# A two-layer stream encoder on one core: the end of the last token tile, with x loaded earlier on another queue, the sample's tokens on four quadrants, and the last stores on other queues

## The chip, the cores and the metric

The kernel runs on one core of a Trainium2 chip. The metric is the device time of one execution in microseconds. The core's engines appear in the profile as PE (TensorE, with PEld for its weight loads), DVE (VectorE), ACT (ScalarE), POOL (GpSimd) and SP (SyncE, which here only issues transfers). All arithmetic is in float32; a matrix product is made of three products of split halves.

## The reference, cut to what matters

Two layers (a gated chunk mixer, then a pooling mixer), each followed by a squared-ReLU channel MLP. The same weights serve 1024 prompt tokens and 32 sample tokens of width 1024; the MLP is 4096 wide. The end of the second layer is what the change touches.

```
h = rmsnorm(x, g_norm[i, 2]) * (1 + sc2) + sh2
f = square(relu(h @ ffn_w_up[i])) @ ffn_w_down[i]
x = x + gt2 * rmsnorm(f, g_norm[i, 3])          # the output, after the last layer
```

## The kernel before, in words

The tokens lie in three tiles: 0 and 1 have 384 prompt tokens each, tile 2 has 256 prompt tokens and the 32 of the sample, 288 columns. Activations are channel-major: `acc[t]` is 128 partitions x 8 channel blocks x the tile's tokens, and `A(t, d)` is one block of it.

The MLP's 4096 hidden channels go in eight chunks of 512. `ffn_item(p, t, after)` is one chunk for one tile. It has four `up(j)`, each a PSUM tile `pf` of 24 products, ReLU and square on ACT, and a split into `fh` (ACT) and `fl` (DVE); and a `down()` with eight groups `pg`, d = 0 to 7, of 12 products each. `accumulate(t, d, ...)` adds each group to `acc` on DVE. `pf` has two PSUM banks (`ps_up`), `pg` three (`ps_dn`), the small sums have `ps_ms`. A `down()` is held back (`pending`) until the next item's first `up` is out. In the last layer the chunks 4 and 5 run over all tiles, then 6 and 7 over tiles 0 and 1, then 6 and 7 over tile 2 alone, so the kernel ends with chunk 7 of tile 2. Weights are loaded on SP's queue into three `raw` buffers, copied by ACT to the high part (`wh`, L422) and subtracted by DVE to the low part (`wl`, L79, the line of the helper behind every DVE add, subtract and multiply-add).

In chunk 7 each accumulated block is squared (`Stat.square`, L750) for the norm. Tiles 0 and 1 are then finished by fillers, generators that a planner (`weave`) advances between groups while its sum of DVE times is behind its sum of PE times: `residual` scales and adds x (`xo_r`), then eight DVE transposes of 32x32 blocks go to `turned` (L1617), each followed by four stores of 48 KB (L1619). Of these q = 3 is on POOL's queue, the others are on SP's.

Tile 2 has an end of its own. `scale_last(d)` multiplies block d by the gate's coefficient on ACT (L1360); at d = 0 it issues nine loads of the tile's x on SP's queue (L1349), from `xsd`, a copy in DRAM, into the room `l0`; and at d = 3, 4, 5 it turns x on DVE (L1355) into the room `h0`, which `turned0` had before. `turn_last(d)` transposes block d on PE (L1368) into `yT`: the two prompt blocks of 128 tokens, and a third that ends with the sample's 32. Behind the last group `last()` makes the norm's sums in `pn_last` with the squares as weights (L1574), then 1/sqrt with one Newton step in three small DVE operations, and six multiply-adds out = yT * r + x, four of 128x512 and two of 32x512. After each comes its store on SP's queue (L1602).

A scheduler puts the instructions of each engine into one fixed list when the program is built; on the chip each engine runs its list in order. Transfers issued by SP and ACT share eight completion semaphores, handed round in the order of the list, and a transfer waits until the one that had its semaphore before it has landed.

Of the kernel before, what the change touches and what calls it, by code (L numbers as in the profile page):

```python
# [15 lines left out]
P = 128  # L16
# [18 lines left out]
def tile_stream_encoder_step(  # L35
# [1088 lines left out]
    def accumulate(t, d, ps, first):  # L1124
        n = ncol[t]
        if first:
            act(out=A(t, d), in_=ps[:, :n], func=AF.Copy)
        else:
            tt(out=A(t, d), in0=A(t, d), in1=ps[:, :n], op=ALU.add)

    def up_terms(wkey, t):
        wh, wl = need_w(wkey)
# [150 lines left out]
    def ffn_item(p, t, after):  # L1283
        l, c, tiles = passes[p]
        last = t == tiles[-1]
        n = ncol[t]
        hid = []

        def up(j):
            ps = ps_up(f"pf{l}_{c}_{t}_{j}")  # L1290
            products(ps, n, up_terms(("up", p, j), t))
            if last:
                w_finish(("up", p, j))
            r = t_m(f"r{l}_{c}_{t}_{j}")
            act(out=r[:, :n], in_=ps[:, :n], func=AF.Relu)  # L1295
            a, b = t_hid("h", f"fh{l}_{c}_{t}_{j}"), t_hid("l", f"fl{l}_{c}_{t}_{j}")
            act(out=r[:, :n], in_=r[:, :n], func=AF.Square)
            split(a, b, r, n)
            hid.append((a, b))

        def down():
            for d in range(KB):
                ps = ps_dn(f"pg{l}_{c}_{t}_{d}")
                wh, wl = need_w(("dn", p, d // 2))
                terms = []
                for j in range(4):
                    o = j * 256 + (d % 2) * P
                    a, b = hid[j]
                    terms.append((wh[:, o : o + P], wl[:, o : o + P], a[:, :n], b[:, :n]))
                products(ps, n, terms)  # L1310
                accumulate(t, d, ps, c == 0)
                if d == 0 and after is not None:
                    st = Stat(t, f"rf{l}_{t}", l == 0 or t < NT - 1)
                if after is not None:
                    st.square(d)
                    if l == 1 and t == NT - 1:
                        scale_last(d)
                        if d in (2, 4, 6):
                            turn_last(d - 2)
                            turn_last(d - 1)  # L1320
                if last and d % 2 == 1:
                    w_finish(("dn", p, d // 2))
                weave(d % 2)
            if after is not None:
                after(st)

        for j in range(4):
            up(j)
            weave()
            if j == 0:  # L1330
                flush()
        pending.append(down)
# [1 line left out]

    last_ps = {}

    def scale_last(d):
        t = NT - 1
        if d == 0:
            last_ps["x"], last_ps["raw"] = (  # L1340
                room(part, 0, f"xlast_{part}").rearrange("p k n -> p (k n)").rearrange(
                    "p (b d) -> p b d", d=D
                )
                for part in "hl"
            )
            src = xsd.rearrange("c k q n -> c (k q) n")
            for i, (c0, r0, nr) in enumerate(LAST):
                for r1 in range(r0, r0 + nr, DEC):
                    nc.sync.dma_start(  # L1349
                        last_ps["raw"][r1 : r1 + DEC, i, :].rearrange("p (m n) -> p m n", n=DEC),  # L1350
                        src[:, :, c0 + r1 : c0 + r1 + DEC],
                    )
        if d in (3, 4, 5):
            i, r0, nr = d - 3, LAST[d - 3][1], LAST[d - 3][2]
            nc.vector.transpose(  # L1355
                out=last_ps["x"][r0 : r0 + nr, i, :], in_=last_ps["raw"][r0 : r0 + nr, i, :]
            )
        for c0, w, v in segs[t]:
            a = A(t, d, c0, w)
            act(out=a, in_=a, func=AF.Copy, scale=coef[:, 1, 3, v, d : d + 1])  # L1360

    def turn_last(d):
        half = d // 4
        for i, (c0, _, _) in enumerate(LAST):
            if d % 4 == 0:
                take = ps_up if half == 0 and i < 2 else (ps_ms if half == 0 or i < 2 else ps_dn)
                last_ps[(i, half)] = take(f"yT{i}_{half}")
            nc.tensor.transpose(  # L1368
                last_ps[(i, half)][:, (d % 4) * P : (d % 4 + 1) * P], A(NT - 1, d, c0, P), ident
            )  # L1370

    def mix_to_ffn(st, l):
        t = st.t
# [182 lines left out]
    def to_out(st):  # L1556
        t = st.t
        col0, npr, nsm = TILES[t]
        blocks = [
            (c * P, P, y_prompt[0, col0 + c * P : col0 + (c + 1) * P, :]) for c in range(npr // P)  # L1560
        ]
        if nsm:
            blocks.append((npr, nsm, y_sample[0]))

        def last():

            turn_last(KB - 2)
            pn = ps_dn("pn_last")
            nb = len(LAST)
            for k in (0, KB - 1):  # L1570
                if k > 0:
                    turn_last(KB - 1)
                for i, (c0, _, _) in enumerate(LAST):
                    mm(  # L1574
                        pn[:, 2 * i : 2 * i + 2],
                        st.sq[:, k, c0 : c0 + P],
                        ones[:, 0:2],
                        start=k == 0 and i == 0,
                        stop=k > 0 and i == nb - 1,
                        skip_group_check=True,  # L1580
                    )
            sums = pn[:, : 2 * nb].rearrange("p (b c) -> p b c", c=2)[:, :, 0]
            r, q = (t_st(f"{x}_last")[:, :nb] for x in ("r", "q"))
            act(out=r, in_=sums, func=AF.Abs_reciprocal_sqrt, scale=1.0 / D)
# [4 lines left out]
            dsts = [dst for _, _, dst in blocks]  # L1589
            for i, (_, r0, nr) in enumerate(LAST):  # L1590
                rows = slice(r0, r0 + nr)
                for half in range(2):
                    d = slice(half * 512, half * 512 + 512)
                    stt(
                        out=xt[rows, i, d],
                        in0=last_ps[(i, half)][rows, :],
                        scalar=r[rows, i : i + 1],
                        in1=xt[rows, i, d],
                        op0=ALU.mult,
                        op1=ALU.add,  # L1600
                    )
                    nc.sync.dma_start(dsts[i][:, d], xt[rows, i, d])  # L1602
            yield False

        def run():
            need_ada(1, 5)
            if t == NT - 1:
                yield from last()
                return
            yield from residual(st, 1, 3, f"r2_1_{t}", [], store=False, stat=False)  # L1610
            turned = room("h", t, f"turned{t}")
            dst = y_prompt[0, col0 : col0 + npr, :].rearrange(
                "(b i) (k q c) -> q k i b c", i=DEC, q=P // DEC, c=DEC
            )
            for k in range(KB):
                time["dve"] += 0.1 + npr / 930.0
                nc.vector.transpose(out=turned[:, k, :], in_=A(t, k))  # L1617
                for q in range(P // DEC):
                    (nc.gpsimd if q == 3 else nc.sync).dma_start(  # L1619
                        dst[q, k],  # L1620
                        turned[DEC * q : DEC * (q + 1), k, :].rearrange("p (b c) -> p b c", c=DEC),
                    )
                yield False

        fillers.append((f"out_{t}", run()))
# [48 lines left out]
```

## Time and profile before

| | us |
|---|---|
| median of three runs | 2172.68 (2172.60, 2172.68, 2174.59) |
| profiled execution | 2173.74 |
| its span | 2171.7 |
| mean granted clock of TensorE | 0.996 |
| busy: PE, DVE, ACT, POOL | 2145.5, 1431.8, 971.3, 13.3 |
| last product of the MLP starts | 2158.75 |
| last multiply-adds start | 2167.11 |

The profiled execution's own time has 2.04 us outside the span, and lies 1.06 above the median. All positions are microseconds from the span's start, in that one execution. In a timeline row the columns are start, duration, engine, line, operation, out<-in with shapes, and the count of instructions that the row joins; a bracket gives the idle time before it and what ended it.

### The profile page before, as it was taken

How to read it: one execution, taken by the hardware profiler on the slowest of the kernel's cores; microseconds unless marked ns; L12 is line 12 of the kernel's file. 1: busy time of each engine (PE TensorE's matmuls, PEld its weight loads, DVE VectorE, ACT ScalarE, POOL GpSimd, SP SyncE). 2: the span in 40 equal slices, each digit the busy share in tenths (PEclk: the TensorE clock that was granted, in tenths of full speed). 3: DMA queues.
4: the chain of work that ended last, by engine and by line, in shares of the span. 5: the costliest groups of instructions: out<-in, count | busy, mean ns of one | idle time of the engine just before them, and what ended most of it. 6: DMA issues, size and time to landing. Idle time of an engine off the chain costs nothing.

```text
span 2171.7 us, 33210 instructions
## 1 busy us (share of the span) xinstructions
PE 2145.5 (99%) x13214; PEld 2078.1 (96%) x13214; DVE 1431.8 (66%) x2499; ACT 971.3 (45%) x1643; POOL 13.3 (1%) x30
## 2 busy tenths in 40 slices
PE   7999999999999999999999999999999999999998
PEld 5778899999999999999999999999999999999997
DVE  5688647566879548496747879869675554523377
ACT  4633422234447552323445566666555542313354
POOL 0000000000000000000000000000000000000001
PEclk9999999999999999999999999999999999999999
DMA  8386534343437454243645466565455552302255
GB/s 300 119 269 193 173 93 139 90 148 109 147 96 233 132 155 143 87 140 110 196 129 161 141 189 182 171 191 158 141 161 158 157 155 68 98 20 78 69 139 125
DMA packets 383262, 312.95 MB, mean 144 GB/s; under 512 B 39458, under 2 KB 346346, under 8 KB 383108
## 3 DMA queue, kind: packets, MB, share of 16 engines
q1 hardware_dynamic: 380452, 308.64, 46.8%
q8 instruction: 103, 1.69, 0.3%
q10 hardware_dynamic: 2144, 1.41, 0.2%
q0 software_dynamic: 512, 0.79, 0.1%
q14 instruction: 51, 0.42, 0.1%
HBM read 278.95 MB, written 31.84 MB: 143 GB/s over the span
## 4 chain that ended last, share of the span: by engine, by line
PE 93%; DVE 3%; DMA 2%; ACT 1%; issue 1%; ACTq 0%; DVEq 0%; SPq 0%
PE pg L902 11%; PE pg L903 11%; PE pg L904 11%; PE pf L902 11%; PE pf L904 11%; PE pf L903 11%; PE po L902 3%; PE po L903 3%; PE po L904 3%; PE pu L902 3%; PE pu L904 3%; PE pu L903 3%; PE pv L929 2%; PE pv L930 2%; PE pv L931 2%; PE pp L1532 1%
## 5 line engine op out<-in xcount | busy, mean ns | idle before, releaser
L902 PE MATMUL pg<-fh,wh_dn 128*128 128x384 f32 (+1 forms) x1536 | 495.8, 323 | 0.0
L902 PE MATMUL pf<-hh,wh_up 128*128 128x384 f32 (+1 forms) x1536 | 494.4, 322 | 0.0
L903 PE MATMUL pf<-hl,wh_up 128*128 128x384 f32 (+1 forms) x1536 | 493.1, 321 | 0.0
L904 PE MATMUL pf<-hh,wl_up 128*128 128x384 f32 (+1 forms) x1536 | 492.9, 321 | 0.2 <-DVE wl_up L79 0.2
L903 PE MATMUL pg<-fl,wh_dn 128*128 128x384 f32 (+1 forms) x1536 | 492.6, 321 | 0.4 <-DVE fl L79 0.4
L904 PE MATMUL pg<-fh,wl_dn 128*128 128x384 f32 (+1 forms) x1536 | 492.5, 321 | 0.0
L79 DVE TENSOR_TENSOR wl_up<-raw,wh_up 128x1024 fp32r<-128x1024 f32 x152 | 185.9, 1224 | 165.4 <-ACT wh_up L422 165.4
L902 PEld LDWEIGHTS pg<-fh,wh_dn 128*128 128x128 f32 x1536 | 288.3, 188 | 1.5 <-ACT fh L1121 0.6
L903 PEld LDWEIGHTS pg<-fl,wh_dn 128*128 128x128 f32 x1536 | 288.3, 188 | 1.5 <-DVE fl L79 0.7
L904 PEld LDWEIGHTS pf<-hh,wl_up 128*128 128x128 f32 x1536 | 288.6, 188 | 0.5 <-DVE wl_up L79 0.5
L903 PEld LDWEIGHTS pf<-hl,wh_up 128*128 128x128 f32 x1536 | 288.3, 188 | 0.4
L902 PEld LDWEIGHTS pf<-hh,wh_up 128*128 128x128 f32 x1536 | 288.2, 188 | 0.4
L904 PEld LDWEIGHTS pg<-fh,wl_dn 128*128 128x128 f32 x1536 | 288.3, 188 | 0.0
L422 ACT ACTIVATE wh_up<-raw 128x1024 fp32r<-128x1024 f32 x152 | 161.2, 1060 | 279.9 <-PE pf L903 213.6
L79 DVE TENSOR_TENSOR acc<-acc,pg 128x384 f32<-128x384 f32 (+1 forms) x336 | 174.2, 519 | 146.3 <-PE pg L904 145.7
L422 ACT ACTIVATE wh_dn<-raw 128x1024 fp32r<-128x1024 f32 x152 | 160.8, 1059 | 202.9 <-PE pg L903 170.6
L79 DVE TENSOR_TENSOR wl_dn<-raw,wh_dn 128x1024 fp32r<-128x1024 f32 x152 | 186.0, 1224 | 82.4 <-ACT wh_dn L422 82.2
L79 DVE SCALAR_TENSOR_TENSOR aa<-raw,csil,aa 128x512 f32<-128x512 f32 (+1 forms) x364 | 203.5, 623 | 8.0 <-DMA raw<-in_w_ada_dram 7.9
L1295 ACT ACTIVATE r<-pf 128x384 f32<-128x384 f32 (+1 forms) x192 | 86.6, 451 | 201.9 <-PE pf L904 199.2
L79 DVE TENSOR_TENSOR fl<-r,fh 128x384 fp32r<-128x384 f32 (+1 forms) x192 | 100.3, 523 | 85.4 <-ACT fh L1121 84.3
L902 PE MATMUL pu<-hh,wh_u 128*128 128x384 f32 (+1 forms) x384 | 125.8, 328 | 0.0
L902 PE MATMUL po<-ush,wh_o 128*128 128x384 f32 (+1 forms) x384 | 123.5, 322 | 0.0
(263 smaller groups left out, 2927.2 us busy)
## 6 DMA issues: line engine op xcount, KB each, us to landing
raw<-in_ffn_w_up_dram SPq DMA_DIRECT2D x152, 512.0 KB, 3.9
raw<-in_ffn_w_down_dram SPq DMA_DIRECT2D x152, 512.0 KB, 3.5
raw<-in_w_ada_dram SPq DMA_DIRECT2D x96, 512.0 KB, 4.3
raw<-in_sgu_w_in_dram SPq DMA_DIRECT2D x40, 512.0 KB, 4.4
xd<-acc SPq DMA_DIRECT2D x8, 1536.0 KB, 7.8
raw<-in_sgu_w_out_dram SPq DMA_DIRECT2D x24, 512.0 KB, 4.0
xo_r<-xd SPq DMA_DIRECT2D x32, 384.0 KB, 3.4
vd<-vt SPq DMA_DIRECT2D x32, 256.0 KB, 4.5
```

The lines of the kernel that those rows point to most:

```text
L79: return op(out, *args, **kw)
L422: act(out=wh, in_=r, func=AF.Copy)
L902: mm(ps[:, :n], wh, rh, start=i == 0, stop=False)
L903: mm(ps[:, :n], wh, rl, start=False, stop=False)
L904: mm(ps[:, :n], wl, rh, start=False, stop=i == last)
L929: mm(ps[:m, :], a_h, wh[:, o : o + 512], start=k == 0, stop=False)
L930: mm(ps[:m, :], a_h, wl[:, o : o + 512], start=False, stop=False)
L931: mm(ps[:m, :], a_l, wh[:, o : o + 512], start=False, stop=k == KB - 1)
L1295: act(out=r[:, :n], in_=ps[:, :n], func=AF.Relu)
L1532: mm(ps[:, :n], wg[:, k, e * P : (e + 1) * P], A(t, 2 * g + k), start=k == 0, stop=k == 1)
```

## The change

- `load_last(j)` is new: in chunk 6 of tile 2, after each `up(j)`, ACT's queue issues three of twelve loads of x (eight of 32 blocks, four of 8 blocks for the sample) into the room `l0`. The sample's 32 tokens are laid out on four quadrants of 32 partitions, 256 channels each.
- x is turned into the room `l1` instead of `h0`, by three DVE transposes (128x1024 twice, 128x256) that are set behind the accumulations d = 1, 2, 3.
- `turn_last` transposes two blocks of 128 tokens instead of three; the sample's 32 columns become weights of a matmul with the identity, which lands on quadrant d // 2 of one PSUM tile `yTs`.
- The norm's sums for the sample are made on each of the four quadrants, and its two multiply-adds of 32x512 become one of 128x256. The last block is turned behind the sums of both squares (k = 0 and 7) instead of between them.
- The scaling of the block d = 7 is on DVE instead of ACT.
- The four large last stores are on ACT's queue; the sample's are four of 32x256, alternately on SP's and ACT's.
- Tile 0's stores of q = 2 move from SP's queue to POOL's.

The core of the diff:

```diff
-    LAST = [(0, 0, P), (P, 0, P), (ncol[-1] - P, P - DEC, DEC)]
+    LAST = (0, P)
...
     def accumulate(t, d, ps, first):
...
+        return tt(out=A(t, d), in0=A(t, d), in1=ps[:, :n], op=ALU.add)
...
-                accumulate(t, d, ps, c == 0)
+                done = accumulate(t, d, ps, c == 0)
...
-                        scale_last(d)
+                        scale_last(d, done.ins)
...
         for j in range(4):
             up(j)
+            if l == 1 and c == 6 and t == NT - 1:
+                load_last(j)
             weave()
...
+    def load_last(j):
+        if j == 0:
+            last_ps["raw"] = room("l", 0, "xlast_l").rearrange("p k n -> p (k n)")
+        raw = last_ps["raw"]
+        src = xsd.rearrange("c k q n -> c (k q) n")
+        parts = [
+            (i * D, DEC, r1, slice(0, DEC), c0 + r1)
+            for i, c0 in enumerate(LAST)
+            for r1 in range(0, P, DEC)
+        ]
+        parts += [
+            (2 * D, 8, DEC * g, slice(8 * g, 8 * g + 8), TILES[-1][1]) for g in range(P // DEC)
+        ]
+        for at, m, r1, ms, n0 in parts[3 * j : 3 * j + 3]:
+            nc.scalar.dma_start(
+                raw[r1 : r1 + DEC, at : at + m * DEC].rearrange("p (m n) -> p m n", n=DEC),
+                src[:, ms, n0 : n0 + DEC],
+            )
...
+    def scale_last(d, done):
         t = NT - 1
         if d == 0:
...
-                    nc.sync.dma_start(
-                        last_ps["raw"][r1 : r1 + DEC, i, :].rearrange("p (m n) -> p m n", n=DEC),
-                        src[:, :, c0 + r1 : c0 + r1 + DEC],
-                    )
-        if d in (3, 4, 5):
...
+            last_ps["x"] = room("l", 1, "xlast_h").rearrange("p k n -> p (k n)")
+        if d in (1, 2, 3):
+            c = slice((d - 1) * D, min(d * D, 2 * D + 256))
+            with tc.issue_after(done):
+                nc.vector.transpose(out=last_ps["x"][:, c], in_=last_ps["raw"][:, c])
+        if d == KB - 1:
+            for c0, w, v in segs[t]:
+                a = A(t, d, c0, w)
+                ts(a, a, coef[:, 1, 3, v, d : d + 1], None, op0=ALU.mult)
+            return
...
     def turn_last(d):
...
+        if d == 0:
+            last_ps["s"] = ps_ms("yTs")
+        q = d // 2 * DEC
+        mm(
+            last_ps["s"][q : q + DEC, d % 2 * P : d % 2 * P + P],
+            A(NT - 1, d, TILES[-1][1], DEC),
+            ident,
+            start=True,
+            stop=True,
+            tile_position=(0, q),
+            skip_group_check=True,
+        )
...
             for k in (0, KB - 1):
-                if k > 0:
-                    turn_last(KB - 1)
-                for i, (c0, _, _) in enumerate(LAST):
+                for i in range(2):
                     mm(
                         pn[:, 2 * i : 2 * i + 2],
...
+                for q in range(0, P, DEC):
+                    mm(
+                        pn[q : q + DEC, 4:6],
+                        st.sq[:, k, npr:],
+                        ones[:, 0:2],
+                        start=False,
+                        stop=k > 0,
+                        tile_position=(0, q),
+                        skip_group_check=True,
+                    )
+            turn_last(KB - 1)
...
+            for i in range(2):
                 for half in range(2):
...
-                    nc.sync.dma_start(dsts[i][:, d], xt[rows, i, d])
+                    nc.scalar.dma_start(blocks[i][2][:, d], x)
+            x = xt[:, 2 * D : 2 * D + 256]
+            stt(
+                out=x,
+                in0=last_ps["s"][:, :256],
+                scalar=r[:, 2:3],
+                in1=x,
+                op0=ALU.mult,
+                op1=ALU.add,
+            )
+            for g in range(P // DEC):
+                (nc.scalar if g % 2 else nc.sync).dma_start(
+                    blocks[2][2][:, g * 256 : (g + 1) * 256], x[DEC * g : DEC * (g + 1), :]
+                )
...
-                    (nc.gpsimd if q == 3 else nc.sync).dma_start(
+                    (nc.gpsimd if q > 1 + t else nc.sync).dma_start(
```

More of the change, by code (lines that the diff above doesn't have):

```diff
@@ L1126, in accumulate @@
         if first:
-            act(out=A(t, d), in_=ps[:, :n], func=AF.Copy)
-        else:
-            tt(out=A(t, d), in0=A(t, d), in1=ps[:, :n], op=ALU.add)
+            return act(out=A(t, d), in_=ps[:, :n], func=AF.Copy)
+        return tt(out=A(t, d), in0=A(t, d), in1=ps[:, :n], op=ALU.add)
     def up_terms(wkey, t):
@@ L1363, in turn_last @@
         half = d // 4
-        for i, (c0, _, _) in enumerate(LAST):
+        for i, c0 in enumerate(LAST):
             if d % 4 == 0:
-                take = ps_up if half == 0 and i < 2 else (ps_ms if half == 0 or i < 2 else ps_dn)
-                last_ps[(i, half)] = take(f"yT{i}_{half}")
+                last_ps[(i, half)] = (ps_up if half == 0 else ps_ms)(f"yT{i}_{half}")
             nc.tensor.transpose(
```

37 lines of the change are left out of this document (10 added, 27 removed).

## The prediction

> **What bounds the kernel now.** I read the page first: its busy times, then the chain that ended last.
>
> ```profile
> span 2171.7 us, 33210 instructions
> PE 2145.5 (99%) x13214; PEld 2078.1 (96%) x13214; DVE 1431.8 (66%) x2499; ACT 971.3 (45%) x1643; POOL 13.3 (1%) x30
> PE 93%; DVE 3%; DMA 2%; ACT 1%; issue 1%; ACTq 0%; DVEq 0%; SPq 0%
> ```
>
> TensorE (PE) is busy for 99% of the span and carries 93% of the chain. So an edit counts only where it makes PE wait, or behind PE's last product. The change touches the last 90 us, so next come windows of that stretch. The columns are the length, then the busy time and count of PE, PEld, DVE, ACT and POOL, then clock, DMA share and GB/s.
>
> ```profile
> 2085.00:2108.40 23.40, 23.40 (x142) 23.40 (x141) 22.80 (x36) 13.42 (x24) 0.00 (x0) 1.00 0.68 191
> 2108.40:2127.50 19.10, 19.10 (x145) 19.10 (x145) 15.48 (x26) 12.04 (x20) 5.07 (x8) 1.00 0.90 216
> 2127.50:2143.70 16.20, 16.20 (x124) 16.20 (x123) 14.56 (x27) 4.57 (x9) 1.50 (x3) 1.00 0.43 95
> 2143.70:2159.00 15.30, 15.30 (x118) 14.87 (x118) 10.04 (x19) 10.31 (x25) 3.45 (x6) 1.00 0.69 119
> 2159.00:2171.70 12.70, 2.15 (x19) 1.82 (x17) 7.58 (x12) 1.34 (x4) 0.00 (x0) 0.65 0.25 93
> ```
>
> PE is full to 2159.0 at 0.13 us a product (19.10 / 145, 288 columns each). DVE is nearly full to 2143.7 and looser after. The last 12.7 us are a tail in which PE does little. The timeline of that tail:
>
> ```profile
> 2158.75 0.29 PE L904 MATMUL pg<-fh,wl_dn 128*128 128x288 f32 x1
> 2159.08 0.45 DVE L79 TENSOR_TENSOR acc<-acc,pg 128x288 f32<-128x288 f32 x1 [0.81 <-PE pg L904]
> 2159.21 1.69 PE L1574 MATMUL pn_last<-ones,sq_rf 128*128 128x2 f32 x12
> 2160.93 0.17 ACT L1584 ACTIVATE r_last<-pn_last 128x3 f32<-128x3 f32 x1 [0.17 <-PE pn_last L1574]
> 2161.80 1.41 DVE L79 SCALAR_TENSOR_TENSOR xlast_h<-yT,r_last,xlast_h 128x512 f32<-128x512 f32 x2
> 2163.13 1.23 DVE L1355 STREAM_TRANSPOSE xlast_h<-xlast_l 128x1024 f32<-128x1024 f32 x1
> 2164.40 1.41 DVE L79 SCALAR_TENSOR_TENSOR xlast_h<-yT,r_last,xlast_h 128x512 f32<-128x512 f32 x2
> 2165.84 1.24 DVE L1355 STREAM_TRANSPOSE xlast_h<-xlast_l 32x1024 f32<-32x1024 f32 x1
> 2167.11 1.44 DVE L79 SCALAR_TENSOR_TENSOR xlast_h<-yT,r_last,xlast_h 32x512 f32<-32x512 f32 x2
> ```
>
> After PE's last product come one accumulation, the norm, and then six final multiply-adds with two transposes of x between them, all on DVE: 2161.80 to 2168.55, that is 6.75 us. The last store and the close take the remaining 3.15 us.
>
> **The tail on DVE: -3.7 us.** The two transposes (1.27 us each by starts) move ahead of the last product, and the sample's two multiply-adds on 32 partitions become one on 128x256. The four big ones keep 0.665 us each ((2163.13 - 2161.80) / 2). The 128x256 one is estimated at 0.42, below the 0.53 that 384 columns take in the next fence. Sum 4 x 0.665 + 0.42 = 3.08 instead of 6.75. Bounds -3.5 and -3.8, by that one estimate.
>
> **DVE before the last product: +2.0 us.** The transposes are not free where they go. Worse, the order of PE's products changes. In the list of the changed kernel, the chunk 6 down groups of the last tile are interleaved with chunk 7's up groups, and the first of the eight groups becomes complete only 141 products after 2108.41, at about 2127.5 (141 x 0.132 plus pauses). DVE's next instruction is that group's accumulation, so DVE stands idle from about 2122.1, with the weights' low parts (wl_up, wl_dn) and tile 1's residual queued behind it. What it then does, by start-to-start times:
>
> ```profile
> 2129.65 0.45 DVE L79 TENSOR_TENSOR acc<-acc,pg 128x288 f32<-128x288 f32 x1
> 2130.02 0.55 DVE L79 SCALAR_TENSOR_TENSOR r_rf<-q_rf,r_rf 128x384 f32<-128x384 f32 x1
> 2130.49 1.22 DVE L79 TENSOR_TENSOR wl_dn<-raw,wh_dn 128x1024 fp32r<-128x1024 f32 x1
> 2131.62 0.45 DVE L79 TENSOR_TENSOR acc<-acc,pg 128x288 f32<-128x288 f32 x1
> 2131.99 1.15 DVE L79 SCALAR_TENSOR_TENSOR acc<-acc,coef,r_rf 128x384 f32<-128x384 f32 x2
> 2133.05 0.45 DVE L79 TENSOR_TENSOR acc<-acc,pg 128x288 f32<-128x288 f32 x1
> 2136.35 0.95 DVE L79 TENSOR_TENSOR acc<-acc,xo_r 128x768 f32<-128x768 f32 x1
> 2137.22 1.14 DVE L79 SCALAR_TENSOR_TENSOR acc<-acc,coef,r_rf 128x384 f32<-128x384 f32 x2
> 2140.05 2.41 DVE L1617 STREAM_TRANSPOSE turned<-acc 128x384 f32<-128x384 f32 x5
> 2146.46 0.46 DVE L79 TENSOR_TENSOR acc<-acc,pg 128x288 f32<-128x288 f32 x1 [0.62 <-PE pg L904]
> ```
>
> Each 288-column add takes 0.37, a 1024-column subtract 1.13, a 384-column multiply-add 0.53, a 768-column add 0.87 and a turned transpose 0.48. The changed list has, from 2127.5 to chunk 7's first accumulation, 12, 6, 10, 4 and 2 of these: 4.4 + 6.8 + 5.3 + 3.5 + 1.0 = 21.0 us. With 0.8 for waits the first accumulation ends at 2149.3; before, it started at 2146.46 and was over at 2146.83. DVE is 2.5 late. Next it has, up to the fourth accumulation, three adds (1.1), six turned transposes (2.9), two x transposes (2.4) and 0.3 of squares: the fourth ends at about 2156.0. The seventh down group uses the bank that the fourth frees (three banks), so PE waits there, some 0.5 us after 0.8 earlier. Then come 24 products (3.2) and three turn groups (1.8): last product over at 2160.9 instead of 2158.9. Bounds: -0.3 if DVE keeps up, since PE's own turning gets a little shorter, and +3.0 if DVE needs 1 us more.
>
> A turn group was three transposes, and is now two with two passes of the sample's 32-token matmul on a quadrant. What a passage into quadrants and back costs is shown where eight quadrant matmuls stand between products:
>
> ```profile
> 1904.15 0.34 PE L904 MATMUL pg<-fh,wl_dn 128*128 128x384 f32 x1
> 1904.42 0.26 PE L459 MATMUL ada<-sums,squares 128*32 128x16 f32 x8
> 1904.61 0.45 PE L902 MATMUL pg<-fh,wh_dn 128*128 128x384 f32 x1
> 1904.90 0.34 PE L903 MATMUL pg<-fl,wh_dn 128*128 128x384 f32 x1
> 2156.64 0.82 PE L1368 MATMUL yT<-ident,acc 128*128 128x128 f32 x6
> 2157.21 0.38 PE L902 MATMUL pg<-fh,wh_dn 128*128 128x288 f32 x1
> ```
>
> From 1904.15 to 1904.90 it is 0.75 us, of which two products take 0.34; the group with its two passages takes 0.41, about 0.1 a passage. Six transposes took 0.57 (2156.64 to 2157.21), so 0.095 each. A turn group: 0.19 + 0.2 + 0.2 = 0.6, against 0.29 before. The Trainium skill, "TensorEngine Tiling (Array Packing)", section "Tiling Modes", says that changing the tiling mode drains TensorE. That speaks against this change, and the longer gaps around 1904.42 agree; it has no figure, and with passages at nothing the sum would be 0.2 us lower for each turn group behind the wait.
>
> **The norm: +0.5 us.** Ahead of the second half of the norm (the last square's), PE now has the seventh channel block's turn group and a first half with two full and four quadrant matmuls. That is some 0.6 + 0.3 + 0.5 = 1.4 us, where PE waits about 1.0 us for accumulation and square (2159.08 to about 2160.1). So 0.4 to 0.5 sticks out; bounds 0.2 and 0.9. Scaling the eighth block on DVE instead of ACT lies beside this.
>
> **The stores: +4.4 us.** This is the largest and least visible term. The kernel's hardware transfers share eight completion semaphores handed round in list order, and each transfer waits for the one before it on its semaphore. In the changed list, five of tile 1's last turned stores, on SP, come behind ACT's final stores, and so wait until those have landed. Those on SP behind them, and two of the sample's four stores, wait too.
>
> ```profile
> out_dram<-turned SPq DMA_DIRECT2D x48, 48.0 KB, 3.0
> out_dram<-xlast_h SPq DMA_DIRECT2D x4, 256.0 KB, 2.0
> L1619 SPq DMA_DIRECT2D out_dram<-turned x48: 315/468/1712, 2109.9 to 2157.4; - x48
> L1602 SPq DMA_DIRECT2D out_dram<-xlast_h x6: 332/340/357, 2162.6 to 2168.6; - x6
> L1619 POOL DMA_DIRECT2D out_dram<-turned x16: 615/615/748, 2110.2 to 2154.2; - x16
> ```
>
> (The first two rows end in us to landing; the others have the issue in ns, min/median/max, and the first and last start.) Before, the last turned store was issued at 2157.4, well ahead of the final ones. Afterwards, let S be the start of the first final multiply-add. The second big store is issued at S + 1.5 and lands 2.0 later, at S + 3.5. Only then do seven turned stores go out, 0.47 to 0.5 apart: the seventh at S + 6.55, the two sample stores at 7.05 and 7.4. From the last issue to the end it was 3.1 (2168.6 to 2171.7), so the end is at S + 10.5; the seventh's own landing in 3.0 gives up to 10.95. I take 10.6. The last multiply-add ends at S + 3.08, so 7.5 follow where 3.15 did: +4.4. Issues at the least value, 0.315, make it +3.3; the late landing makes it +4.8.
>
> **At nothing.** The twelve loads of x go to ACT's queue in chunk 6:
>
> ```profile
> L1146 ACTq DMA_DIRECT2D bs<-in_sgu_b_s_dram x12: 330/334/347, 7.4 to 566.3; - x12
> L1349 SPq DMA_DIRECT2D xlast_l<-xsd x9: 543/589/774, 2079.0 to 2145.6; - x9
> ```
>
> An issue costs 0.33 to 0.77, so 4 to 9 us together. ACT is busy for 13.42 of the 23.40 us there, so 10 are free. The squares of the hidden layer queue behind the issues; if one came late, PE would wait up to 0.8, and I find none that does. Tile 0's third-quadrant stores move from SP to POOL: 24 x 0.615 = 14.8 us on an engine with nothing else in its window, over before the end. Below nothing: SP has fewer issues, but it waits for DVE's turned data anyhow.
>
> **Sum.** 2.0 + 0.5 - 3.7 + 4.4 = +3.2. The profiled execution took 2173.74 us, span 2171.7 and 2.04 around it, so it would be 2176.9; it lies 1.06 above the median of the runs, 2172.68, and from there I predict 2175.9. What a measurement can tell from no change is about 0.2%, 4.35 us: faster is below 2168.3, slower above 2177.0.
>
> **Rivals.** First, slower: DVE's queue becomes the bound outright. The times above are start to start, where one instruction overlaps the next; the durations shown are about 0.08 longer. If waits between engines break the overlap for 20 of the 34 instructions, DVE comes 1.6 later, and every microsecond goes to PE at the fourth accumulation: +4.8, or 2177.5, and to 2178.5 with the stores at their bound. It decides once the fourth accumulation ends 1.15 us behind my 2156.0. For it speaks DVE's 14.56 of 16.20 us busy; against it, that in such a stretch before the starts do follow closely. Second, a gain: the turned stores get out before the final ones, because the semaphores don't bind as I read them. Then the last sample store goes out 0.4 behind the last multiply-add, its term is +0.4 instead of +4.4, and the sum is -0.8: 2171.9. Against it stands the order in the list. Third, this and DVE keeping up (-0.3 instead of +2.0): -3.1, or 2169.6; DVE, busy for 10.04 of 15.30 us after 2143.7, would have to take in the whole 2.5 there. That the change doesn't do what it says (x still turned late) would put 2.5 back onto the tail while the stores keep their cost: 2178.4, inside the first rival's price; the list has the transposes ahead of the fifth accumulation.
>
> **How the numbers follow.** Forecast 0.55, first rival 0.28 with the late x in it, gain 0.12, third 0.05. Of the third about half lies below 2168.3: faster 0.03. Slower is 0.26 of the first rival and 0.05 of the forecast's upper part: 0.31. The rest, 0.66, is within 0.2%. The range runs from the gain's lower side, 2171.6, to the first rival's upper one, 2178.6.
>
> **What would show it.** Right: PE without a gap to about 2143, then waits of 0.3 to 1 us at down groups released by DVE's accumulation; DVE idle near 2122 to 2127; the final multiply-adds within 3.1 us with no transposes between; turned stores issued on SP behind the final stores on ACT, and over 7 us from the last multiply-add to the end. Wrong: turned stores all issued before the first final one (the gain), PE's last product before 2159.5, or after 2162 (the first rival).

## The result, and the profile after

| | kernel before | changed kernel |
|---|---|---|
| median of 12 runs, us | 2171.73 | 2177.10 |
| profiled execution, its span | 2173.74, 2171.7 | 2181.23, 2179.0 |

The ratio of the two is 1.0024, with a 95% interval from 1.0016 to 1.0033: the change makes the kernel slower by 5.2 us (3.5 to 7.2), clear of noise but small, about 0.24%. Both profiled executions lie above their medians, that of the changed kernel by 4.1 us. Part of this was there before any changed line ran. The chain of work and the rows of one ReLU that both kernels make (the first `up` of chunk 7 for tile 1) show it. First the page of the changed kernel:

```profile
span 2179.0 us, 33250 instructions
PE 2146.7 (99%) x13234; PEld 2077.0 (95%) x13234; DVE 1429.8 (66%) x2500; ACT 968.5 (44%) x1641; POOL 18.3 (1%) x38
PE 91%; DVE 4%; DMA 3%; ACT 1%; issue 1%; ACTq 0%; DVEq 0%; SPq 0%
```

Then that ReLU, in the timeline of the kernel before and of the changed one:

```profile
2060.10 0.47 ACT L1295 ACTIVATE r<-pf 128x384 f32<-128x384 f32 x1
```

```profile
2062.86 0.47 ACT L1294 ACTIVATE r<-pf 128x384 f32<-128x384 f32 x1
```

At that point the second execution is 2.76 us late already, with the same work behind it. So all stages below are counted from this ReLU. The tail of the changed kernel, in the timeline:

```profile
2165.21 0.29 PE L904 MATMUL pg<-fh,wl_dn 128*128 128x288 f32 x1
2165.54 0.46 DVE L79 TENSOR_TENSOR acc<-acc,pg 128x288 f32<-128x288 f32 x1 [1.67 <-PE pg L904]
2167.51 0.17 ACT L1616 ACTIVATE r_last<-pn_last 128x3 f32<-128x3 f32 x1 [1.04 <-PE pn_last L1604]
2168.38 2.73 DVE L79 SCALAR_TENSOR_TENSOR xlast_h<-yT,r_last,xlast_h 128x512 f32<-128x512 f32 x4
2169.17 2.31 ACTq L1633 DMA_DIRECT2D out_dram<-xlast_h  x4
2171.03 0.48 DVE L79 SCALAR_TENSOR_TENSOR xlast_h<-yTs,r_last,xlast_h 128x256 f32<-128x256 f32 x1
2171.58 0.90 ACTq L1644 DMA_DIRECT2D out_dram<-xlast_h  x2
2171.89 3.64 SPq L1663 DMA_DIRECT2D out_dram<-turned  x7
2175.63 0.91 SPq L1644 DMA_DIRECT2D out_dram<-xlast_h  x2
```

The final multiply-adds are short, 3.13 us (2168.38 to 2171.51), and no transpose stands between them. But behind them SP issues seven turned stores of tile 1, whose data DVE had finished turning by 2158.9, and only then its two sample stores. The waits of SP's queue name the reason (columns: us in total, times, longest):

```profile
SPq L1663 <- DMA out_dram<-xlast_h: 11.0, 1, 11.0
```

A turned store waited 11.0 us for a final store to land. The four stages of both kernels, worked out from the starts of these rows:

| us | ReLU to last product | to first final multiply-add | multiply-adds | to the span's end | sum |
|---|---|---|---|---|---|
| before | 98.65 | 3.05 | 6.75 | 3.15 | 111.60 |
| changed | 102.35 | 3.17 | 3.13 | 7.49 | 116.14 |
| difference | +3.70 | +0.12 | -3.62 | +4.34 | +4.54 |
| predicted | +2.0 | +0.5 | -3.7 | +4.4 | +3.2 |

Three of the four terms came out as forecast within 0.4 us, the first was nearly double. The stages' sum of +4.54 leaves 0.7 of the measured 5.2 unexplained; it lies ahead of the ReLU or is scatter. The runs were to show what that term is made of, and whether the stores' term is really a wait on shared semaphores.

### The profile page after: what moved, and what is told of

It is laid out like the page before. It is cut to its first block, busy times and chain, and to the rows that moved or that the text cites. A ratio compares the mean times of both kernels' runs of the same rounds, so it can differ in the third digit from the quotient of the medians.

```text
span 2179.0 us, 33250 instructions
## 1 busy us (share of the span) xinstructions
PE 2146.7 (99%) x13234; PEld 2077.0 (95%) x13234; DVE 1429.8 (66%) x2500; ACT 968.5 (44%) x1641; POOL 18.3 (1%) x38
## 4 chain that ended last, share of the span: by engine, by line
PE 91%; DVE 4%; DMA 3%; ACT 1%; issue 1%; ACTq 0%; DVEq 0%; SPq 0%
PE pg L902 11%; PE pg L904 11%; PE pg L903 11%; PE pf L902 11%; PE pf L904 11%; PE pf L903 11%; PE po L902 3%; PE po L903 3%; PE po L904 3%; PE pu L902 2%; PE pu L904 2%; PE pu L903 2%; PE pv L929 2%; PE pv L930 2%; PE pv L931 2%; DMA raw<-in_w_ada_dram 2%
```

## The experiments

Each was timed in five rounds beside the kernel before. "Sum" is that of the four stages from the profile of one execution each; the measured difference is that of the medians. Where PE's list is the same, the stage to the last product repeats within 0.1 from run to run (102.35 and 102.26; 98.44, 98.44 and 98.43).

| run | to last product | to multiply-adds | multiply-adds | to end | sum against before | measured, ratio |
|---|---|---|---|---|---|---|
| all last stores on SP | 102.26 | 3.18 | 3.12 | 4.30 | +1.26 | +1.57, 1.0007 (0.9999 to 1.0016) |
| and no quadrants | 100.10 | 3.06 | 4.19 | 2.86 | -1.39 | -1.94, 0.9990 (0.9982 to 0.9999) |
| only the stores' queues | 98.44 | 3.06 | 4.19 | 7.42 | +1.51 | +1.87, 1.0010 (1.0001 to 1.0019) |
| quadrants batched | 101.88 | 3.21 | 3.12 | 4.35 | +0.96 | +0.74, 1.0003 (0.9994 to 1.0012) |
| only POOL's line | 98.44 | 3.06 | 4.19 | 2.83 | -3.08 | -2.83, 0.9983 (0.9974 to 0.9991) |
| no quadrants, loads on SP in chunk 6 | 106.71 | 3.06 | 4.19 | 2.78 | +5.14 | +4.96, 1.0020 (1.0011 to 1.0028) |
| the same, sample on ACT and POOL | 105.68 | 3.06 | 2.73 | 3.77 | +3.64 | +4.94, 1.0022 (1.0013 to 1.0031) |
| no quadrants, loads on SP in chunk 7 | 98.48 | 4.33 | 4.19 | 2.76 | -1.84 | -1.84, 0.9991 (0.9982 to 1.0000) |
| quadrants, loads on SP in chunk 7 | 100.84 | 3.55 | 3.12 | 4.30 | +0.21 | +0.33, 1.0003 (0.9994 to 1.0012) |
| POOL's line and half the sample off DVE | 98.43 | 3.06 | 3.52 | 2.97 | -3.62 | -2.68, 0.9989 (0.9980 to 0.9998) |

**All last stores on SP.** From the changed kernel:

```diff
-                    nc.scalar.dma_start(blocks[i][2][:, d], x)
+                    nc.sync.dma_start(blocks[i][2][:, d], x)
...
-                (nc.scalar if g % 2 else nc.sync).dma_start(
+                nc.sync.dma_start(
```

> The changed kernel with all last stores (four of 128x512, four of the sample) on SP's queue again, nothing else undone. Theory: the late end is the wait of tile 1's turned stores for the final stores that ACT issues ahead of them on the same semaphores; with one queue these turned stores stand ahead in the list, so they go out before the first final multiply-add, no wait of SP for a final store is left, and from the last multiply-add's end to the end of the span it is about 4.2 us instead of 7.5 (3.15 as before, and three more issues of 0.34 for the sample): 3.3 us faster than the changed kernel, some 1 to 2 us slower than the kernel before. Rival: the turned stores are late because DVE turns them late; then they still go out behind the final ones and the time stays as it was, about 5 us above the kernel before.

In its timeline the turned stores are out before the final multiply-adds begin, and the final stores follow at once:

```profile
2146.11 13.47 SPq L1663 DMA_DIRECT2D out_dram<-turned  x24
2163.38 2.73 DVE L79 SCALAR_TENSOR_TENSOR xlast_h<-yT,r_last,xlast_h 128x512 f32<-128x512 f32 x4
2164.16 2.31 SPq L1633 DMA_DIRECT2D out_dram<-xlast_h  x4
2166.55 1.81 SPq L1644 DMA_DIRECT2D out_dram<-xlast_h  x4
```

The end follows the last multiply-add by 4.30 us instead of 7.49, -3.2 where -3.3 was expected. The stage ahead of the last product stayed (102.26 against 102.35). So the wait belongs to the choice of queues; DVE's turning was never late. The rival falls.

**No quadrants.** The run before, with the sample turned by a third transpose a block, as in the kernel before; x is still loaded and turned early.

```diff
-        for i, c0 in enumerate(LAST):
+        for i, c0 in enumerate((0, P, ncol[-1] - P)):
...
-        mm(
-            last_ps["s"][q : q + DEC, d % 2 * P : d % 2 * P + P],
...
-            for g in range(P // DEC):
+            for half in range(2):
+                x = xt[P - DEC :, 2 * D + half * 512 : 2 * D + half * 512 + 512]
```

> As the run with all last stores on SP, and the sample's tokens turned by three transposes a block as in the kernel before (two final multiply-adds of 32x512), while x is still loaded and turned early. Theory: the passages of PE into quadrants and back cost 0.43 us for each of the six blocks turned before the last product, so PE ends 2.2 to 2.6 us earlier; the tail on DVE grows by 2 x 0.72 - 0.48 = 0.95, and there are two sample stores instead of four (-0.7): about 2 us faster than with quadrants, which is at or 1 us below the kernel before. Rival: DVE, being late, sets PE's end; then PE ends where it did and the run is 0.3 us slower to the same as the one with quadrants.

PE's last product came 2.16 us earlier (100.10 against 102.26), the multiply-adds took 4.19 instead of 3.12, the end was 1.44 shorter with two stores fewer. That is -2.65 in the stages and -3.5 in the medians: the quadrants cost more ahead of the last product and in stores than the one multiply-add saves. The gain is larger than the 2 us expected, since the two stores less gave 1.44 and not 0.7. DVE does not set PE's end alone.

**Only the stores' queues**, from the kernel before:

```diff
-                    nc.sync.dma_start(dsts[i][:, d], xt[rows, i, d])
+                    (nc.scalar if i < 2 or half else nc.sync).dma_start(dsts[i][:, d], xt[rows, i, d])
...
-                    (nc.gpsimd if q == 3 else nc.sync).dma_start(
+                    (nc.gpsimd if q > 1 + t else nc.sync).dma_start(
```

> The kernel before with the change of queues alone: tile 0's third store of each block on POOL, the four large last stores and the second of the sample's two on ACT's queue, the first of the sample's on SP. Theory: in the list ACT's final stores again stand ahead of the last twelve turned stores, one of which waits for the sample's store on ACT that goes out behind the very last multiply-add (about 2168.7, landing 1.7 to 2.0 later); four turned stores (0.47 each), one sample store and 3.1 to the end follow: the end is 4 to 4.5 us later than in the kernel before. Rival: moving stores between queues costs nothing by itself: within 0.5 us of the kernel before.

The time missed both expectations: +1.9. The profile shows why. In the waits and in the timeline of this run:

```profile
SPq L1619 <- DMA out_dram<-xlast_h: 14.0, 1, 14.0
```

```profile
2158.49 4.19 DVE L79 SCALAR_TENSOR_TENSOR xlast_h<-yT,r_last,xlast_h 128x512 f32<-128x512 f32 x6
2167.22 0.41 SPq L1602 DMA_DIRECT2D out_dram<-xlast_h  x1
```

The stores' term is there as expected (7.42 against 3.15 to the end, +4.27, with a wait of 14.0). But the six final multiply-adds now run without a break: the two x transposes have left the tail, though no line about them was changed. I had not foreseen that; it gives back 2.56.

**Quadrants batched.** The run with all last stores on SP, and the sample's matmuls of blocks 0 to 5 together behind block 5:

```diff
-        q = d // 2 * DEC
-        mm(
+        for e in {5: range(6), 6: (6,), 7: (7,)}.get(d, ()):
+            q = e // 2 * DEC
+            mm(
```

> As the run with all last stores on SP, but the sample's quadrant matmuls of the blocks 0 to 5 stand together behind the transposes of block 5 instead of one group behind each block. The same matmuls, five pairs of passages less. Theory: the passages are what makes a turn group dear (0.76 us beside two product intervals, of which two transposes take 0.19 and the matmuls themselves some 0.3): PE's last product comes 1.0 to 1.5 us earlier. Rival: the matmuls themselves are dear, or DVE sets the end: within 0.3 us of the run with all last stores on SP.

The timeline has the batch, and a wait ahead of it:

```profile
2155.12 0.40 PE L902 MATMUL pg<-fh,wh_dn 128*128 128x288 f32 x1 [0.77 <-DVE acc L79]
...
2157.61 0.64 PE L1386 MATMUL yTs<-ident,acc 128*32 128x128 f32 x10
2158.18 0.40 PE L904 MATMUL pg<-fh,wl_dn 128*128 128x288 f32 x1
...
2158.55 0.38 PE L1379 MATMUL yT<-ident,acc 128*128 128x128 f32 x2
2158.86 0.41 PE L1386 MATMUL yTs<-ident,acc 128*32 128x128 f32 x2
```

The scheduler put ten of the twelve passes into the batch and the last block's two behind that block's own transposes, so the run makes four passages less, not five. Ten passes took 0.57 us from their first start to the next product, where a pair takes 0.34 (2161.27 to 2161.61 in the changed kernel, shown in the next section). So a pass costs 0.03, and 0.28 of the pair's time is passage. That counts only from the first pass on. Ahead of it, 0.30 us go from the start of the two transposes to the first pass (2160.97 to 2161.27), and two transposes take 0.19 elsewhere, by the prediction's row of six; so a passage in and out is about 0.4 in all, an estimate. The four passages less fit it: the turning ahead of the last product fell by 1.8 us, 0.46 for each. Yet the last product came only 0.4 earlier, short of the 1.0 to 1.5 expected, because PE then waited for DVE: its pauses at products rose by 1.5, the 0.77 shown among them. That wait is at the seventh down group, the place that the prediction had named. So here DVE's lateness took back most of what PE saved; the run without quadrants, whose list of PE's products differs a little, kept its 2.16.

**Only POOL's line**, from the kernel before:

```diff
-                    (nc.gpsimd if q == 3 else nc.sync).dma_start(
+                    (nc.gpsimd if q > 1 + t else nc.sync).dma_start(
```

> The kernel before with one line changed: tile 0's third store of each block goes to POOL's queue. Theory: eight issues less on SP let the scheduler place the two late x transposes ahead of the last product (as the run with the change of queues alone showed, 4.19 us of final multiply-adds instead of 6.75 without any early load), and with the last stores all on SP nothing is taken back: 2.5 to 2.9 us faster than the kernel before. Rival: that order came from the final stores on ACT; then the two transposes stay in the tail and the time is that of the kernel before within 0.5 us.

This settles the miss of the run on queues. The two transposes stand ahead of the norm, and the final multiply-adds again run through:

```profile
2154.20 1.24 DVE L1355 STREAM_TRANSPOSE xlast_h<-xlast_l 128x1024 f32<-128x1024 f32 x1
2156.54 1.24 DVE L1355 STREAM_TRANSPOSE xlast_h<-xlast_l 32x1024 f32<-32x1024 f32 x1
2158.78 4.19 DVE L79 SCALAR_TENSOR_TENSOR xlast_h<-yT,r_last,xlast_h 128x512 f32<-128x512 f32 x6
2159.56 3.78 SPq L1602 DMA_DIRECT2D out_dram<-xlast_h  x6
```

Eight stores fewer on SP, and the list of DVE's instructions is another; -2.83 us of time (0.9983, 0.9974 to 0.9991), what moving the two transposes out of the tail was to bring, and nothing taken back.

**Loads on SP in chunk 6**, from the run without quadrants:

```diff
-            nc.scalar.dma_start(
+            nc.sync.dma_start(
                 raw[r1 : r1 + DEC, at : at + m * DEC].rearrange("p (m n) -> p m n", n=DEC),
```

> As the run without quadrants, with the twelve early loads of x (nine here) on SP's queue instead of ACT's, in the same place of chunk 6. Theory: it is the loads on ACT that make the scheduler interleave chunk 6's down groups with chunk 7's up groups; on SP the list of PE's products is that of the kernel before, DVE is not left idle near 2124 to 2130, and PE's waits between products fall from 2.5 to about 0.9 us: 1.4 us faster than the run without quadrants, 2.8 to 3.2 below the kernel before. Rival: the early transposes on DVE are what makes PE wait; then it is as the run without quadrants within 0.4 us.

Both theories fell: 6.9 us slower than with the loads on ACT. PE's products are again listed as in the kernel before, but DVE's list is not. The timeline of DVE and PE:

```profile
2154.76 3.33 DVE L1638 STREAM_TRANSPOSE turned<-acc 128x384 f32<-128x384 f32 x7
2158.00 0.42 DVE L79 TENSOR_TENSOR acc<-acc,pg 128x288 f32<-128x288 f32 x1
2158.48 0.61 PE L902 MATMUL pg<-fh,wh_dn 128*128 128x288 f32 x1 [4.93 <-DVE acc L79]
```

Four adds of x (`xo_r`) for tile 1 and all eight of its turned transposes stand between the third accumulation of chunk 7 and the fourth, which holds a bank that PE needs: PE waits 4.93 us. Why the list has them so late is argued, not shown: SP's queue, with the nine loads in chunk 6, has the loads of `xo_r` behind more transfers, and what hangs on them is listed later on DVE.

**The sample on ACT and POOL**, from that run:

```diff
-                stt(
...
+                act(out=y, in_=last_ps[(2, half)][P - DEC :, :], func=AF.Copy, scale=r[P - DEC :, 2:3])
+                nc.gpsimd.tensor_tensor(out=x, in0=x, in1=y, op=ALU.add)
```

> As the run with the loads on SP, and the sample's two final multiply-adds of 32x512 taken off DVE: ACT scales the turned block by r, POOL adds x. Theory: ACT and POOL are idle there and take 2 x 0.55 and 2 x 0.6 to 1.0 us while DVE does its four (2.7 us), so the multiply-adds end 1.4 us earlier and the run is 1.2 to 1.5 us faster than the one with the loads on SP, some 4 us below the kernel before. Rival: POOL's adds take over 1.3 us each, so that the sample's stores become last; then the gain is below 0.5 us or turns into a loss.

```profile
2167.89 1.25 ACT L1616 ACTIVATE xlast_l<-yT,r_last 32x512 f32<-32x512 f32 x2 [0.70 <-DVE r_last L79]
2167.90 2.73 DVE L79 SCALAR_TENSOR_TENSOR xlast_h<-yT,r_last,xlast_h 128x512 f32<-128x512 f32 x4
2168.71 2.49 POOL L1617 TENSOR_TENSOR xlast_h<-xlast_h,xlast_l 32x512 f32<-32x512 f32 x2 [3.94 <-ACT xlast_l L1616]
```

An add on POOL takes 1.24, near the rival's 1.3, and the two end 0.57 behind DVE's last. Multiply-adds and end together take 6.50 instead of 6.97, so 0.47 is won in the tail, within the rival's 0.5 and not the 1.2 to 1.5 of the theory. The medians (+4.94 against +4.96) don't show it. The stage ahead of the last product is 1.03 shorter too, though no line there was changed: behind the same pause of PE the slow clock, of which the last section tells, lasted for 3.6 us here and 6.2 there.

**Loads on SP in chunk 7**, without and with quadrants. From the runs without quadrants and with all last stores on SP, the same edit in both:

```diff
-            if l == 1 and c == 6 and t == NT - 1:
-                load_last(j)
...
+            for j in range(4):
+                load_last(j)
...
-            nc.scalar.dma_start(
+            nc.sync.dma_start(
```

> As the run without quadrants, but the nine loads of x are on SP's queue in chunk 7 as in the kernel before, not in chunk 6. Theory: loads in chunk 6, on either queue, change the lists of PE or DVE for the worse (by PE's order on ACT's queue, by the late residual on SP's); here both lists are those of the kernel before up to chunk 7, PE's waits between products are 0.7 to 0.9 us, and the time is that of the run with POOL's queue alone within 0.4 us, 2.8 below the kernel before. Rival: what makes PE wait is the other new work ahead of the last product (the eighth block's scaling on DVE, transposes bound to accumulations): then it stays near the run without quadrants, 1.4 to 1.9 below the kernel before.

> The same with the sample on four quadrants: the changed kernel with all last stores on SP and the loads of x on SP in chunk 7. Theory: with DVE in time the passages cost PE 0.43 us for each of the six blocks ahead of the last product, 2.6 us; the final multiply-adds take 3.12 instead of 4.19, and four sample stores instead of two put 1.4 behind them: about 2.9 us slower than the run without quadrants and with the same loads. Rival: PE has slack there once DVE is in time, and the quadrants cost nothing ahead of the last product: 0.4 us slower or less.

These two and the two with loads on ACT make a square of the stage ahead of the last product:

| us, ReLU to last product | loads on ACT in chunk 6 | loads on SP in chunk 7 | the loads' share |
|---|---|---|---|
| quadrants | 102.26 | 100.84 | 1.42 |
| no quadrants | 100.10 | 98.48 | 1.62 |
| the quadrants' share | 2.16 | 2.36 | |

Each cause costs nearly the same with and without the other. With late loads and no quadrants the stage is that of the kernel before (98.65). In the traces the order of PE's up and down products is that of the kernel before in both runs with the loads on SP in chunk 7, and interleaved in all that have them on ACT in chunk 6; with the order, the pauses of PE that DVE ends are gone.

The first run's tail is 1.27 longer than with POOL's line alone, since one transpose of x came between the three small operations of the norm on DVE (4.33 instead of 3.06). So the time stayed at -1.84, which is the number of the rival and not of the theory; but the stage in question, 98.48 against 98.44, went as the theory said, and the rival's cause is not there. The second run was expected 2.9 slower than the first; it is 2.2 slower by the medians and 2.05 by the stages: +2.36 ahead of the last product, -0.78 in the norm, -1.07 in the multiply-adds and +1.54 behind them. That is the theory's side, with a shorter transpose in the norm, which it did not foresee.

**POOL's line and half the sample off DVE**, from the run with POOL's line alone:

```diff
+                    if i == 2 and half == 0:
+                        y = last_ps["raw"][rows, i, d]
+                        act(out=y, in_=last_ps[(i, half)][rows, :], func=AF.Copy, scale=r[rows, i : i + 1])
+                        nc.gpsimd.tensor_tensor(out=xt[rows, i, d], in0=xt[rows, i, d], in1=y, op=ALU.add)
+                    else:
```

> The run with POOL's queue alone, and the first of the sample's two final multiply-adds made by ACT (scaling by r, 0.63) and POOL (adding x, 1.24), beside DVE's four large ones; the second stays on DVE. Theory: DVE's tail falls from 4.19 to 3.46 us and nothing else moves: 0.6 to 0.8 us faster than with POOL's queue alone, 3.4 to 3.6 below the kernel before. Rival: POOL's or ACT's access beside DVE's slows DVE's multiply-adds, or the sample's first store delays the second on SP; then no gain.

```profile
2159.61 3.52 DVE L79 SCALAR_TENSOR_TENSOR xlast_h<-yT,r_last,xlast_h 128x512 f32<-128x512 f32 x5
2160.42 1.26 POOL L1597 TENSOR_TENSOR xlast_h<-xlast_h,xlast_l 32x512 f32<-32x512 f32 x1 [10.82 <-ACT xlast_l L1596]
```

The stages give 0.54 less than POOL's line alone (107.98 against 108.52), where 0.6 to 0.8 was expected. The times don't tell the two apart (ratios 0.9989 and 0.9983 with overlapping intervals). Either beats both kernels; the one-line version is the simpler.

## Why the prediction was right, and where it was not

The time came within 1.2 us of the forecast (2177.10 against 2175.9), and part of that is luck: the forecast stood on a median of three runs, 2172.68, and twelve runs have 2171.73. The difference that was forecast, +3.2, came as +5.2, so it is 2.0 short. The terms one by one:

**The tail on DVE** (-3.7, came -3.62): the count of instructions and their durations held; the 128x256 multiply-add took 0.48 where 0.42 was estimated. What I did not see is that most of it was to be had otherwise: POOL's line alone removes 2.56 of it. The early loads and the bound transposes bring nothing in the tail beyond that, and the quadrants 1.07 (4.19 to 3.12).

**The stores** (+4.4, came +4.34): shown. The wait of SP is on a final store, 11.0 us; it goes when the queues are undone, and it comes (14.0 us) when the queues alone are changed. The first of the seven turned stores went out at S + 3.51 (2171.89 - 2168.38; S is the start of the first final multiply-add), where S + 3.5 was forecast. The two sample stores behind the turned ones were forecast to go out from S + 7.05 on; they did from S + 7.25 (2175.63 - 2168.38).

**The norm** (+0.5, came +0.12): over-sized. The matmuls that I had sticking out of the wait for the last square by 0.4 to 0.5 us stick out by 0.12 (3.18 with quadrants and 3.06 without, in the two runs with all stores on SP).

**DVE before the last product** (+2.0, came +3.7): this is the term that failed, in its size and in half of its cause. What I said of DVE is there. Its timeline in the changed kernel, with ACT's queue ahead of it:

```profile
2119.51 3.63 ACTq L1352 DMA_DIRECT2D xlast_l<-xsd  x2
2123.18 1.06 ACT L422 ACTIVATE wh_up<-raw 128x1024 fp32r<-128x1024 f32 x1 [3.64 <-issue]
2124.28 1.23 DVE L79 TENSOR_TENSOR wl_up<-raw,wh_up 128x1024 fp32r<-128x1024 f32 x1 [2.34 <-ACT wh_up L422]
2127.46 0.46 DVE L79 TENSOR_TENSOR fl<-r,fh 128x288 fp32r<-128x288 f32 x1 [1.96 <-ACT fh L1121]
2130.43 0.82 DVE L79 TENSOR_TENSOR acc<-acc,pg 128x288 f32<-128x288 f32 x2 [2.51 <-PE pg L904]
```

DVE is idle for most of 2122 to 2130 and starts again at 2130.43, which without the 2.76 us of the early delay is 2127.7, against a forecast of 2127.5. The first accumulation of chunk 7 ended near 2150.0 on the same count (2149.3 was forecast) and the fourth at 2156.5 (2156.0). DVE's lateness did make PE wait, but not where I had put it. The one wait of PE that the profile puts down to DVE is at the fourth down group, for the bank that the first accumulation frees:

```profile
2152.81 0.40 PE L902 MATMUL pg<-fh,wh_dn 128*128 128x288 f32 x1 [0.57 <-DVE acc L79]
```

The seventh group began at 2159.91, 0.6 behind the end of the fourth accumulation (2159.29), so there was no wait there: by then PE was the later of the two.

I had set the loads on ACT's queue at nothing. In fact two of them held ACT for 3.63 us, and `wh_up` with it. The cause is the one that I had seen for the stores and not looked for here: the loads take their turn on the same eight semaphores. In the trace the second of the two waits on the semaphore of a weight load of SP, which landed at 2121.64; its issue starts at 2121.66. Behind two later loads ACT's timeline names tile 0's stores:

```profile
2125.44 0.44 ACT L1296 ACTIVATE r<-r 128x288 f32<-128x288 f32 x1 [0.90 <-DMA out_dram<-turned]
2126.98 0.44 ACT L1121 ACTIVATE fh<-r 128x288 fp32r<-128x288 f32 x1 [1.10 <-DMA out_dram<-turned]
```

These stalls lie in time in which DVE waits for PE anyway, so what they add is not shown. The whole price of the loads on ACT in chunk 6, by the square, is 1.4 to 1.6 us. That it goes when the loads stand elsewhere, and with it the interleaved order of PE's products and the pauses behind it, is shown; how much of it is the order and how much the stalls of ACT is not.

The other 2.2 to 2.4 are PE's own turning, which I charged to three groups only, those behind the wait at the seventh down group, and otherwise held to be covered by DVE's lateness. This is the step that failed: all six groups cost, and each more than I had. A turn group between products, in the timeline of the changed kernel:

```profile
2160.83 0.29 PE L903 MATMUL pg<-fl,wh_dn 128*128 128x288 f32 x1
2160.97 0.38 PE L1379 MATMUL yT<-ident,acc 128*128 128x128 f32 x2
2161.27 0.41 PE L1385 MATMUL yTs<-ident,acc 128*32 128x128 f32 x2
2161.61 0.40 PE L904 MATMUL pg<-fh,wl_dn 128*128 128x288 f32 x1
2161.85 0.29 PE L902 MATMUL pg<-fh,wh_dn 128*128 128x288 f32 x1
```

From 2160.83 to 2161.85 are 1.02 us, of which two products take 0.26: a group costs 0.76 where I had 0.6. In the kernel before, two groups cost 0.66 (2156.51 to 2157.43, for them and two products; the rows between stand in the prediction):

```profile
2156.51 0.29 PE L904 MATMUL pg<-fh,wl_dn 128*128 128x288 f32 x1
...
2157.43 0.30 PE L903 MATMUL pg<-fl,wh_dn 128*128 128x288 f32 x1
```

So a group costs 0.43 more, and all six ahead of the last product pay it: 2.6, of which 2.2 to 2.4 reach the end. The Trainium skill, "TensorEngine Tiling (Array Packing)", section "Tiling Modes", says that a change of the tiling mode drains TensorE; the row agrees, with 0.34 us for two passes of 0.03 each.

**The rivals.** The time came near that of the slower rival (2177.5), but not by its mechanism: DVE came 0.5 us later than forecast at the fourth accumulation, not 1.6. The sign named for it did come, PE's last product after 2162 (2165.21, or 2162.45 without the early delay); PE's own turning can bring that too, so the sign did not tell the two apart. The gain is excluded, since the semaphores did bind, and the third rival with it. Two bounds do not follow from the prediction's own terms: the late landing gives +4.7 (10.95 - 3.08 - 3.15) and not +4.8, and the slower rival with the stores at +4.8 gives 2177.9 and not 2178.5. The two terms that nearly cancel, tail and stores, were sized right, and the sign of the sum came from them and the third, as forecast.

## What to carry to other kernels

When transfers share completion semaphores in the order of one list, a late store on a second queue can hold back earlier work on the first: before moving a store, look at what stands behind it in that list, and in the profile at waits of one queue on another's stores. The same holds for loads on the queue of an engine that computes: there the wait stops the engine itself. A transfer that is moved also changes the order that a scheduler gives to compute engines, so compare the lists of all engines and not only the queue in question; here one line that lightened SP's queue brought 2.8 us, most of the 3.7 that the larger change meant to bring to the tail. Small matmuls in another tiling mode, strewn between full ones, pay for each passage: batch them, or let them be full ones.

## What the runs showed of the hardware that I had not expected

The passage into a quadrant's tiling and back costs about 0.4 us, over ten times a pass of 128 columns in it (0.03): 0.28 from the first pass to the next product, and 0.11 ahead of it. And a single long pause of PE is paid twice. In the run with loads on SP in chunk 6, windows behind the pause of 4.93 us read (columns as in the prediction):

```profile
2143.00:2153.00 10.00, 10.00 (x77) 9.71 (x76) 7.64 (x11) 5.27 (x13) 0.00 (x0) 1.00 0.13 34
2153.00:2158.40 5.40, 0.55 (x5) 0.31 (x3) 5.40 (x12) 0.00 (x0) 2.02 (x4) 0.95 0.53 95
2158.40:2166.00 7.60, 7.52 (x36) 7.23 (x37) 4.64 (x11) 4.54 (x12) 2.93 (x5) 0.59 0.78 131
```

The granted clock was 1.00 before the pause and 0.59 in the 7.6 us after it, with 36 matmuls in 7.52 us where 77 had taken 10.00. Closer in, it was 0.50 for 6.2 us (2158.4 to 2164.6), which loses 3.1 us beside the pause's 4.93, an estimate. Together they make up most of the 8.2 us by which this run's last product is later than with the loads in chunk 7 (106.71 against 98.48). The Trainium skill, "TensorE: Matmul & The Clock Gate", states in its part on the clock gate that an idle window of about 3.4 us brings the clock to half; the row agrees in kind.
